# A decoder trunk on one core: the pre-norm's factor of each feature moves from the transposed input into the weights of the feed-forward parts

## The chip, the cores and the metric

The kernel runs on one core of a Trainium2 chip. The metric is the device time of one execution in microseconds, and the time before is the median of three runs. In what follows TensorE, VectorE, ScalarE, GpSimd and SyncE are the five engines of the core; the profile calls them PE (with PEld for its weight loads), DVE, ACT, POOL and SP.

## What is computed

Two layers act on 256 tokens of 1024 features in float32. A layer is a feed-forward part, a token mixer (a short convolution, sparse attention and attention into 256 memory tokens), and a second feed-forward part. The part that matters here is this:

```python
def rms_norm(x, g):
    y = x * lax.rsqrt(jnp.mean(x * x, axis=-1, keepdims=True) + EPS)
    return y * g                       # g: one factor for each of 1024 features

def swiglu(h, w_in, w_out):            # w_in 1024 x 5632, w_out 2816 x 1024
    a, b = jnp.split(h @ w_in, 2, axis=-1)
    return (jax.nn.silu(a) * b) @ w_out

for l in range(2):
    h = rms_norm(x, ffn1_norm_pre[l])
    x = x + 0.5 * rms_norm(swiglu(h, ffn1_w_in[l], ffn1_w_out[l]), ffn1_norm_post[l])
    h = rms_norm(x, mix_norm_pre[l])
    x = x + rms_norm(token_mixer(h, ...), mix_norm_post[l])
    h = rms_norm(x, ffn2_norm_pre[l])
    x = x + 0.5 * rms_norm(swiglu(h, ffn2_w_in[l], ffn2_w_out[l]), ffn2_norm_post[l])
```

The factor `g` multiplies the rows of `w_in` as well as it multiplies the columns of the normed input: `(y * g) @ w_in` is `y @ (g[:, None] * w_in)`.

## The kernel before

**Numbers in two pieces.** Each float32 operand of a matmul is split into a high piece (`hi`, rounded to the format that TensorE multiplies fast) and the rest (`lo`). A product is three matmuls into one PSUM bank: hi by hi, hi by lo, lo by hi. For weights this is `split_unit` (L280): ScalarE copies the loaded tile `raw` to `whi` (L286), and VectorE subtracts, `wlo = raw - whi` (L287). For activations it is done behind a transpose.

**Units of weights.** A unit is one tile of 128 partitions by 1024 columns (512 KB). In the feed-forward input product (`product`, L348) a unit is one k of eight (128 of the 1024 features) with 512 columns of `a` and 512 of `b`; five groups of columns are done so. The last 256 + 256 columns go through `halves` (L367): there a unit holds two k at once, so that it is again 1024 columns wide, and four units make the product. It uses `product2` (L361), which takes the two k one behind the other.

**Two streams.** The 256 tokens are two streams of 128, t = 0 and t = 1. Each runs through the layers in steps, and a loop (L1309) lets them step in turn, t = 1 some steps behind, so that both use the same unit of weights. A step of a feed-forward part is six matmuls of 512 columns.

**Order.** The program is run once dry to learn at which step each unit is asked for (its due time). In the real pass `prefetch` (L293) issues a unit's load up to 7 steps ahead of its due time (`LOADS`) and its split up to 4 steps ahead (`AHEAD`), as long as there is a free buffer: 4 for `raw` and 8 for the pairs of `whi` and `wlo`. Every unit counts as one buffer, whatever its width. SyncE's queue keeps this order. On the other engines the framework places instructions by its own planner, in which the order of the program is the priority, and it derives the waits; only in the first steps are instructions pinned to the order of the program (`pinned`, L175).

**The pre-norm.** `prenorm` (L446) transposes a stream's 128 x 1024 input on TensorE, four 128 x 128 blocks to a PSUM bank (`pt`, two banks). VectorE multiplies each half by the factors into `hf` (`gained`, L457), ScalarE copies that to `hThi` (L462), VectorE makes `hTlo` (L463). The reciprocal of the root mean square is applied later, behind the product. The call for the first part of all is `warm` (L465): it interleaves the two halves with the splits of the first two units, and the second half's factors are applied by ScalarE in four pieces (L454). Idle matmuls (`keep_clock`) stand beside it.

**Behind the product** comes `gate` (L537: ScalarE tanh L539, VectorE L540 and L544), and for every two groups of columns a transpose that goes through VectorE, DRAM and back (`turn`, L394), whose end is again a split (`turnhi` L423, `turnlo` L424). Then `output` (L516) multiplies by `w_out`, 22 units of one k by 1024 columns.

Of the kernel before, what the change touches and what calls it, by code (L numbers as in the profile page):

```python
# [24 lines left out]
AF = mybir.ActivationFunctionType  # L25
OP = mybir.AluOpType
AX = mybir.AxisListType

P = 128
# [28 lines left out]
ATT_A, ATT_B, ATT_C, ATT_D, ATT_T = 1, 3, 2, 6, 10  # L58
EARLY, RAMP, SCALES, STAGED = 6, 10, 5, 8
PACE, PACE_1, PACED = 9, 8, ("nsa", "memory")  # L60

PRE = ("ffn1_norm_pre", "mix_norm_pre", "ffn2_norm_pre", "mem_norm")

# [40 lines left out]
def view(ap, off, dims):  # L104
    if isinstance(ap, Nothing):
        return ap
    return bass.AP(tensor=ap.tensor, offset=ap.offset + off, ap=[list(ap.ap[0])] + [list(d) for d in dims])


def f32(ap):  # L110
    return ap.bitcast(F32)
# [19 lines left out]
def program(tc, nc, pools, a, out, plan):  # L131
# [18 lines left out]
    def bank(name):  # L150
        return psa.tile([P, 512], F32, name=name, tag="a")

    def tbank():
        return pst.tile([P, 512], F32, name="pt", tag="t")

    def gtile(name, dt=F32):
        return gp.tile([P, 1024], dt, name=name, tag="g")

    def ttile(name, dt=F32):
        return tp.tile([P, 520], dt, name=name, tag="tmp")  # L160
# [7 lines left out]
    def keep_clock(count):  # L168
        ps = bank("idle")
        for _ in range(count):  # L170
            pinned(nc.tensor.matmul(ps, lhsT=idle[:, :P], rhs=idle[:, :512], start=True, stop=True))
# [3 lines left out]
    def pinned(ins):  # L175
        if first_steps[0] and not dry:
            tc.keep_in_program_order(ins)
# [5 lines left out]
    for half in range(2):  # L183
        sl = slice(half * 512, (half + 1) * 512)
# [9 lines left out]
    gT = consts.tile([P, 64], F32, name="gT")  # L194
# [24 lines left out]
    def ask(kind, key, parts=None):  # L219
        if dry:  # L220
            if key not in found:
                found[key] = [now[0], kind, key, parts, 0]
                order.append(found[key])
            found[key][4] += 1
            return nc if kind == "g" else [nc, nc]
        if key not in ready:
            fetch(key)
        return ready[key]

    def unit(key, parts):  # L230
        hi, lo = ask("w", key, parts)
        later(0, lambda: drop("w", key))
        return hi, lo

    def drop(kind, key):
        if not dry:
            left[key] -= 1
            if left[key] == 0:
                free[kind] += 1
# [39 lines left out]

    def split_unit(between=None):  # L280
        item, raw, n = splits.pop(0)
        free["w"] -= 1
        hi = wp.tile([P, 1024], F32R, name="whi")
        lo = wp.tile([P, 1024], F32R, name="wlo")
        for c0, c1 in ((0, n),) if between is None else ((0, n // 2), (n // 2, n)):
            pinned(nc.scalar.copy(hi[:, c0:c1], raw[:, c0:c1]))  # L286
            pinned(nc.vector.tensor_sub(lo[:, c0:c1], raw[:, c0:c1], f32(hi[:, c0:c1])))  # L287
            if c0 == 0 and between is not None:
                between()
        ready[item[2]] = [hi, lo]  # L290
        free["raw"] += 1
# [41 lines left out]
    def later(delay, fn):  # L333
        serial[0] += 1
        deferred.append((now[0] + delay, serial[0], fn))
# [7 lines left out]
    def mm3(ps, xh, xl, wh, wl, start, stop, skip=False):  # L343
        nc.tensor.matmul(ps, lhsT=xh, rhs=wh, start=start, stop=False, skip_group_check=skip)  # L344
        nc.tensor.matmul(ps, lhsT=xh, rhs=wl, start=False, stop=False, skip_group_check=skip)  # L345
        nc.tensor.matmul(ps, lhsT=xl, rhs=wh, start=False, stop=stop, skip_group_check=skip)  # L346
# [14 lines left out]
    def product2(ps, x2, hi, lo, n, k0, first, last):  # L361
        for kk in range(2):
            k = k0 + kk
            mm3(ps[:, :n], x2[0][:, k], x2[1][:, k], hi[:, kk * n:(kk + 1) * n], lo[:, kk * n:(kk + 1) * n],
                first and kk == 0, last and kk == 1)

    def halves(hT, name, l, parts):  # L367
        ps = bank("acc")
        width = sum(n for _, n in parts)
        for u in range(4):  # L370
            hi, lo = unit((name, l, parts[0][0], u), [(i * n, width, name, l, 2 * u, 2, c, n)
                                                      for i, (c, n) in enumerate(parts)])
            product2(ps, hT, hi, lo, width, 2 * u, u == 0, u == 3)
            yield 0
        return ps
# [9 lines left out]
    def transpose4(src, c0, n=4):  # L385
        pt = tbank()
        for j in range(n):
            pinned(nc.tensor.transpose(pt[:, j * P:(j + 1) * P], src[:, c0 + j * P:c0 + (j + 1) * P], ident))  # L388
        return pt
# [52 lines left out]
    def tokens_last(hi, lo):  # L442
        r = "p (k t) -> p k t"
        return hi.rearrange(r, k=8), lo.rearrange(r, k=8)

    def prenorm(src, name, l, warm=False):  # L446
        hi, lo = gtile("hThi", F32R), gtile("hTlo", F32R)
        g0 = PRE.index(name) * 16 + l * 8
        hf = [ttile("hf") for _ in range(2)]

        def gained(half, pt):
            if warm and half == 1:
                for c in range(4):
                    pinned(nc.scalar.activation(hf[1][:, c * P:(c + 1) * P], pt[:, c * P:(c + 1) * P], AF.Copy,  # L454
                                                scale=gT[:, g0 + 4 + c:g0 + 5 + c]))
                return
            pinned(nc.vector.tensor_tensor(view(hf[half], 0, [[P, 4], [1, P]]), view(pt, 0, [[P, 4], [1, P]]),  # L457
                                           view(gT, g0 + half * 4, [[1, 4], [0, P]]), op=OP.mult))

        def halved(half):  # L460
            sl = slice(half * 512, (half + 1) * 512)
            pinned(nc.scalar.copy(hi[:, sl], hf[half][:, :512]))  # L462
            pinned(nc.vector.tensor_sub(lo[:, sl], hf[half][:, :512], f32(hi[:, sl])))  # L463

        if warm and splits:  # L465
            pts = []
            for half in range(2):
                pts.append(transpose4(src, half * 512))
                keep_clock(WARM[1 + half])
            gained(0, pts[0])  # L470
            split_unit(lambda: halved(0))
            split_unit()
            gained(1, pts[1])
            halved(1)
        else:
            for half in range(2):
                gained(half, transpose4(src, half * 512))
            for half in range(2):
                halved(half)
        scale = norm_scales(src, SCALES if first_steps[0] else 0)  # L480
        yield NORM_B
        return tokens_last(hi, lo), scale
# [731 lines left out]
    def mixer(t, l):  # L1214
# [3 lines left out]
        def columns(c0, n=512):  # L1218
            return halves(hT, "w_mix_in", l, [(c0, n)])
# [147 lines left out]
```

## Time and profile before

| | |
|---|---|
| median of 3 runs | 1257.37 us (1257.1 to 1258.28) |
| the profiled execution | 1259.41 us, of which 1257.7 us are the span from its first to its last instruction |
| TensorE, matmuls | 1242.4 us busy, 99% of the span |
| TensorE, weight loads | 1027.2 us, 82% |
| VectorE | 915.1 us, 73% |
| ScalarE | 725.6 us, 58% |
| GpSimd | 211.8 us, 17% |
| DMA | 286.85 MB, 228 GB/s in the mean |

Busy times are of the whole span. A stage has its own limit, and which wait ends last in a stage is read from its rows. A matmul's duration in the timeline is longer than its share of TensorE's time, since matmuls overlap; the distance from one start to the next is what counts.

### The profile page before, as it was taken

To read this page: it belongs to the slowest core of one execution; us is meant where nothing else is said; L and a number is where in the kernel's file an instruction comes from. 1 tells how busy PE (TensorE), PEld (TensorE's weight loads), DVE (VectorE), ACT (ScalarE), POOL (GpSimd) and SP (SyncE) were. 2 spreads that over 40 slices of the span, in tenths; PEclk is the share of its full clock that TensorE was granted. 3 is DMA by queue.
4 is the path that set the end of the run, shared out by engine and by line. 5 is a ranking of instruction groups with operands and counts; after the bars stand their busy time and mean duration, and the time that the engine had idled before them with its cause. 6 is when DMAs were issued, how large, how long until landed. Compare 5 with 4: busy or idle time off the path is not lost.

```text
span 1257.7 us, 16609 instructions
## 1 busy us (share of the span) xinstructions
PE 1242.4 (99%) x5775; PEld 1027.2 (82%) x5775; DVE 915.1 (73%) x1168; ACT 725.6 (58%) x1138; POOL 211.8 (17%) x413
## 2 busy tenths in 40 slices
PE   9999999999999999999999999999999999999997
PEld 6888888878887888888888888888888888888886
DVE  7767657888997686676576676678899876767753
ACT  6545545877875454554464545568867754645441
POOL 3011601402120011011011014024012200110110
PEclk9999999999999999999999999999999999999999
DMA  7877876776687657787757788758558877577871
GB/s 255 261 242 264 279 246 216 225 232 201 188 272 241 219 175 213 246 255 229 251 173 230 233 271 300 242 178 258 162 192 272 243 235 219 172 244 220 250 248 71
DMA packets 133907, 286.85 MB, mean 228 GB/s; under 512 B 11872, under 2 KB 30976, under 8 KB 133824
## 3 DMA queue, kind: packets, MB, share of 16 engines
q1 hardware_dynamic: 117984, 238.78, 60.9%
q0 software_dynamic: 15520, 46.49, 11.1%
q8 instruction: 45, 0.74, 0.2%
q10 hardware_dynamic: 320, 0.53, 0.1%
q14 instruction: 38, 0.31, 0.1%
HBM read 261.64 MB, written 24.12 MB: 227 GB/s over the span
## 4 chain that ended last, share of the span: by engine, by line
PE 81%; DVE 6%; DMA 5%; ACT 4%; issue 3%; POOL 1%; DVEq 0%; SPq 0%; POOLq 0%; ACTq 0%
PE acc L356 34%; PE y L346 7%; PE y L345 7%; PE y L344 7%; PE acc L346 6%; PE acc L344 6%; PE acc L345 6%; DVE wlo L287 2%; DMA moved<-there 2%; PE pt L388 1%; PE br L344 1%; PE br L346 1%; PE br L345 1%; ACT whi L286 1%; DMA there<-blocks 1%
## 5 line engine op out<-in xcount | busy, mean ns | idle before, releaser
L287 DVE TENSOR_TENSOR wlo<-raw,whi 128x1024 fp32r<-128x1024 f32 (+2 forms) x441 | 532.3, 1214 | 247.1 <-ACT whi L286 242.7
L286 ACT CAST whi<-raw 128x1024 fp32r<-128x1024 f32 (+2 forms) x441 | 456.9, 1043 | 371.3 <-PE acc L356 177.9
L356 PE MATMUL acc<-wlo,hThi 128*128 128x512 f32 x640 | 198.6, 390 | 0.0
L356 PE MATMUL acc<-whi,hThi 128*128 128x512 f32 x640 | 197.8, 391 | 0.3 <-ACT hThi L462 0.3
L356 PE MATMUL acc<-whi,hTlo 128*128 128x512 f32 x640 | 197.2, 389 | 0.0
L344 PE MATMUL acc<-whi,hThi 128*128 128x512 f32 (+1 forms) x480 | 187.5, 391 | 0.4 <-ACT hThi L462 0.4
L346 PE MATMUL acc<-whi,hTlo 128*128 128x512 f32 (+1 forms) x480 | 184.8, 385 | 0.1
L345 PE MATMUL acc<-wlo,hThi 128*128 128x512 f32 (+1 forms) x480 | 184.7, 385 | 0.0
L403 POOL DMA_DIRECT2D there<-blocks x184 | 101.1, 556 | 490.8 <-DVE blocks L398 408.7
L356 PEld LDWEIGHTS acc<-whi,hThi 128*128 128x128 f32 x640 | 119.9, 188 | 25.6 <-ACT hThi L462 0.7
L356 PEld LDWEIGHTS acc<-whi,hTlo 128*128 128x128 f32 x640 | 120.1, 188 | 25.2 <-DVE hTlo L463 0.4
L356 PEld LDWEIGHTS acc<-wlo,hThi 128*128 128x128 f32 x640 | 120.1, 188 | 25.3 <-DVE wlo L287 0.4
L346 PE MATMUL y<-whi,turnlo 128*128 128x512 f32 x352 | 137.3, 390 | 0.0
L345 PE MATMUL y<-wlo,turnhi 128*128 128x512 f32 x352 | 137.2, 390 | 0.0
L344 PE MATMUL y<-whi,turnhi 128*128 128x512 f32 x352 | 137.1, 389 | 0.0
L346 PEld LDWEIGHTS acc<-whi,hTlo 128*128 128x128 f32 x480 | 90.2, 188 | 18.5 <-DVE hTlo L463 0.6
L344 PEld LDWEIGHTS acc<-whi,hThi 128*128 128x128 f32 x480 | 90.3, 188 | 17.3 <-ACT hThi L462 1.3
L345 PEld LDWEIGHTS acc<-wlo,hThi 128*128 128x128 f32 x480 | 90.4, 188 | 15.1
L345 PEld LDWEIGHTS y<-wlo,turnhi 128*128 128x128 f32 x352 | 66.1, 188 | 13.7
L346 PEld LDWEIGHTS y<-whi,turnlo 128*128 128x128 f32 x352 | 66.1, 188 | 13.7
L344 PEld LDWEIGHTS y<-whi,turnhi 128*128 128x128 f32 x352 | 66.1, 188 | 13.6
L424 DVE TENSOR_TENSOR turnlo<-moved,turnhi 128x1024 fp32r<-128x1024 f32 (+1 forms) x42 | 49.2, 1171 | 31.0 <-ACT turnhi L423 31.0
(293 smaller groups left out, 1457.6 us busy)
## 6 DMA issues: line engine op xcount, KB each, us to landing
raw<-in_ffn_w_in_dram SPq DMA_DIRECT2D x159, 512.0 KB, 4.8
raw<-in_w_mix_in_dram SPq DMA_DIRECT2D x96, 512.0 KB, 4.5
raw<-in_ffn_w_out_dram SPq DMA_DIRECT2D x88, 512.0 KB, 4.6
there<-blocks POOLq DMA_DIRECT2D x152, 128.0 KB, 4.5
moved<-there POOLq DMA_DIRECT2D x38, 512.0 KB, 5.8
raw<-in_ffn_w_in_dram SPq DMA_DIRECT2D x33, 256.0 KB, 4.1
raw<-in_w_mem_kv_dram SPq DMA_DIRECT2D x16, 512.0 KB, 5.0
raw<-in_w_mix_out_dram SPq DMA_DIRECT2D x16, 512.0 KB, 4.4
```

What stands on the lines that cost most here:

```text
L286: pinned(nc.scalar.copy(hi[:, c0:c1], raw[:, c0:c1]))
L287: pinned(nc.vector.tensor_sub(lo[:, c0:c1], raw[:, c0:c1], f32(hi[:, c0:c1])))
L344: nc.tensor.matmul(ps, lhsT=xh, rhs=wh, start=start, stop=False, skip_group_check=skip)
L345: nc.tensor.matmul(ps, lhsT=xh, rhs=wl, start=False, stop=False, skip_group_check=skip)
L346: nc.tensor.matmul(ps, lhsT=xl, rhs=wh, start=False, stop=stop, skip_group_check=skip)
L356: pinned(nc.tensor.matmul(p[:, :n], lhsT=hT[x2][:, k], rhs=w[:, j * n:(j + 1) * n], start=(k == 0 and i == 0), stop=(k == 7 and i == 2)))
L388: pinned(nc.tensor.transpose(pt[:, j * P:(j + 1) * P], src[:, c0 + j * P:c0 + (j + 1) * P], ident))
L403: nc.gpsimd.dma_start(there[:, q * f:(q + 1) * f].rearrange("(p j) f -> j p f", j=32), blocks[q * 32:(q + 1) * 32, :n].rearrange("j (p f) ...
L424: nc.vector.tensor_sub(lv, mv, f32(hv))
```

## The change

The factors of the two feed-forward pre-norms are multiplied into `w_in` where its units are split: ScalarE's copy becomes an activation with a factor for each partition, and VectorE's subtraction becomes `raw * factor - whi` in one instruction. For this a unit must hold one k, so the units of `halves` are made half as wide (8 of 512 columns in place of 4 of 1024), with the same matmuls in the same order and a step for every two of them. The feed-forward pre-norms lose `hf`: ScalarE and VectorE split the transposed input straight from PSUM. In the `warm` call the second half is split before the second unit instead of behind it. The mixer's pre-norm stays as it was, apart from code that it doesn't reach.

```diff
+FOLDED = {"ffn1_w_in": "ffn1_norm_pre", "ffn2_w_in": "ffn2_norm_pre"}

     def split_unit(between=None):
         item, raw, n = splits.pop(0)
+        gains = None
+        if item[2][0] in FOLDED:
+            k = PRE.index(FOLDED[item[2][0]]) * 16 + item[2][1] * 8 + item[2][3]
+            gains = gT[:, k:k + 1]
...
         for c0, c1 in ((0, n),) if between is None else ((0, n // 2), (n // 2, n)):
-            pinned(nc.scalar.copy(hi[:, c0:c1], raw[:, c0:c1]))
-            pinned(nc.vector.tensor_sub(lo[:, c0:c1], raw[:, c0:c1], f32(hi[:, c0:c1])))
+            if gains is None:
+                pinned(nc.scalar.copy(hi[:, c0:c1], raw[:, c0:c1]))
+                pinned(nc.vector.tensor_sub(lo[:, c0:c1], raw[:, c0:c1], f32(hi[:, c0:c1])))
+            else:
+                pinned(nc.scalar.activation(hi[:, c0:c1], raw[:, c0:c1], AF.Copy, scale=gains))
+                pinned(nc.vector.scalar_tensor_tensor(lo[:, c0:c1], raw[:, c0:c1], gains, f32(hi[:, c0:c1]),
+                                                      op0=OP.mult, op1=OP.subtract))
...
     def halves(hT, name, l, parts):
         ps = bank("acc")
         width = sum(n for _, n in parts)
+        if name in FOLDED:
+            for k in range(8):
+                hi, lo = unit((name, l, parts[0][0], k), [(i * n, 0, name, l, k, 1, c, n)
+                                                          for i, (c, n) in enumerate(parts)])
+                mm3(ps[:, :width], hT[0][:, k], hT[1][:, k], hi[:, :width], lo[:, :width], k == 0, k == 7)
+                if k % 2:
+                    yield 0
+            return ps
...
     def prenorm(src, name, l, warm=False):
-        hf = [ttile("hf") for _ in range(2)]
+        hf = None if name in FOLDED.values() else [ttile("hf") for _ in range(2)]
         def gained(half, pt):
-            if warm and half == 1:
-                for c in range(4):
-                    pinned(nc.scalar.activation(hf[1][:, c * P:(c + 1) * P], pt[:, c * P:(c + 1) * P], AF.Copy,
-                                                scale=gT[:, g0 + 4 + c:g0 + 5 + c]))
-                return
...
-        def halved(half):
+        def halved(half, pt=None):
             sl = slice(half * 512, (half + 1) * 512)
-            pinned(nc.scalar.copy(hi[:, sl], hf[half][:, :512]))
-            pinned(nc.vector.tensor_sub(lo[:, sl], hf[half][:, :512], f32(hi[:, sl])))
+            src = hf[half][:, :512] if pt is None else pt
+            pinned(nc.scalar.copy(hi[:, sl], src))
+            pinned(nc.vector.tensor_sub(lo[:, sl], src, f32(hi[:, sl])))

         if warm and splits:
...
-            gained(0, pts[0])
-            split_unit(lambda: halved(0))
+            split_unit(lambda: halved(0, pts[0]))
+            halved(1, pts[1])
             split_unit()
-            gained(1, pts[1])
-            halved(1)
+        elif hf is None:
+            for half in range(2):
+                halved(half, transpose4(src, half * 512))
         else:
```

## Rows read from the trace of the kernel before

**Rows 1.** Page, part 1: busy us (share of the span) xinstructions

```profile
PE 1242.4 (99%) x5775; PEld 1027.2 (82%) x5775; DVE 915.1 (73%) x1168; ACT 725.6 (58%) x1138; POOL 211.8 (17%) x413
```

**Rows 2.** Busy us of each engine (x instructions), clock, DMA share, GB/s, one stretch

```profile
100.00:200.00 100.00, 100.00 (x442) 82.45 (x441) 64.95 (x65) 50.39 (x58) 28.23 (x52) 1.00 0.81 271
```

**Rows 3.** Who TensorE waited for, whole span: us in total, times, longest

```profile
PE acc L344 <- ACT hThi L462: 0.4, 2, 0.2
PE acc L356 <- ACT hThi L462: 0.3, 1, 0.3
```

**Rows 4.** Waits of all engines, whole span: us in total, times, longest

```profile
DVE wlo L287 <- ACT whi L286: 242.7, 225, 2.9
ACT whi L286 <- PE acc L356: 177.9, 132, 2.2
```

**Rows 5.** Timeline of TensorE's matmuls in the first steps (start, us)

```profile
9.87 1.06 PE L388 MATMUL pt<-ident,x 128*128 128x128 f32 x8 [0.85 <-DMA x<-in_x_dram]
10.69 0.71 PE L356 MATMUL acc<-whi,hThi 128*128 128x512 f32 x2
...
12.61 0.73 PE L356 MATMUL acc<-whi,hThi 128*128 128x512 f32 x2 [0.28 <-ACT hThi L462]
...
17.39 0.62 PE L356 MATMUL acc<-whi,hThi 128*128 128x512 f32 x2
```

**Rows 6.** Chain that ended last, in order of time, first steps (start, us)

```profile
11.31 0.61 DVE hf L457
...
11.94 0.63 ACT hThi L462
```

**Rows 7.** Timeline of SyncE, first steps, and landing times of L267, first 14 us

```profile
3.04 56.85 SPq L267 DMA_DIRECT2D raw<-in_ffn_w_in_dram  x26
...
DMA to landing us min/median/max: 4.7/6.1/8.6
```

**Rows 8.** Groups by line and shape: count, busy us, mean ns, idle before and releasers

```profile
L287 DVE TENSOR_TENSOR wlo<-raw,whi 128x1024 fp32r<-128x1024 f32 x431 | 525.1, 1225 | 246.3 <-ACT whi L286 241.9 <-PE acc L356 0.5
L286 ACT CAST whi<-raw 128x1024 fp32r<-128x1024 f32 x431 | 450.7, 1053 | 369.6 <-PE acc L356 177.9 <-PE y L346 85.9 <-PE acc L346 48.4
...
L511 DVE SCALAR_TENSOR_TENSOR x<-pn,nr,x 128x512 f32<-128x512 f32 x24 | 17.0, 749 | 1.3 <-POOL nr L439 0.4
...
L457 DVE TENSOR_TENSOR hf<-pt,gT 128x512 f32<-128x512 f32 x23 | 15.2, 686 | 1.5 <-PE pt L388 0.9
...
L925 ACT ACTIVATE p<-p,rg 128x256 f32<-128x256 f32 x32 | 13.7, 505 | 2.2 <-DVE rg L810 2.2
...
L379 ACT CAST mThi<-pt 128x512 fp32r<-128x512 f32 x8 | 4.7, 584 | 2.9 <-PE pt L388 2.9
```

**Rows 9.** TensorE around `halves` of the second feed-forward part, layer 0

```profile
555.97 0.39 PE L344 MATMUL acc<-whi,hThi 128*128 128x512 f32 x1
...
562.76 0.39 PE L344 MATMUL acc<-whi,hThi 128*128 128x512 f32 x1
...
566.85 0.39 PE L344 MATMUL y<-whi,turnhi 128*128 128x512 f32 x1
```

**Rows 10.** ScalarE and VectorE in the same stretch

```profile
561.26 1.05 ACT L423 CAST turnhi<-moved 128x1024 fp32r<-128x1024 f32 x1 [1.78 <-DMA moved<-there]
...
564.32 1.05 ACT L286 CAST whi<-raw 128x1024 fp32r<-128x1024 f32 x1 [0.48 <-PE acc L346]
...
562.35 1.23 DVE L424 TENSOR_TENSOR turnlo<-moved,turnhi 128x1024 fp32r<-128x1024 f32 x1 [1.60 <-ACT turnhi L423]
...
565.34 0.75 DVE L544 SCALAR_TENSOR_TENSOR wide<-th,rs,acc 128x512 f32<-128x512 f32 x1
```

**Rows 11.** SyncE: loads of these units; then their issues, min/median/max ns; then landing

```profile
533.57 9.09 SPq L276 DMA_DIRECT2D raw<-in_ffn_w_in_dram  x8
...
L276 SPq DMA_DIRECT2D raw<-in_ffn_w_in_dram x32: 367/425/1475, 94.7 to 1163.9; - x32
...
raw<-in_ffn_w_in_dram SPq DMA_DIRECT2D x33, 256.0 KB, 4.1
```

## The prediction, made before the change was run

> **What bounds the kernel now.** The page comes first: TensorE's matmuls are busy for 1242.4 of 1257.7 us, VectorE for 915.1, ScalarE for 725.6 [rows 1]. So no engine that the change relieves or loads has to be the bound, and only 15.3 us of the span are without a matmul. The next view, the busy times of a stretch, says whether busy means full: in 100 us of a feed-forward part 442 matmuls start, one every 0.2262 us, with no idle time [rows 2]. I use 0.2262 as the cadence; a step (six matmuls) is 1.357 us, and a unit of weights, used by both streams, lasts 2.71 us.
>
> Then the waits: of the waits of TensorE for what the pre-norm makes (`hThi`), the whole span has 0.3 us in the feed-forward parts (L356) and 0.4 us at L344 [rows 3], which in a feed-forward part is never the first to read it: that is the mixers. The longest waits are of other engines: VectorE for ScalarE's copy, 242.7 us, and ScalarE for TensorE, 177.9 us in 132 waits [rows 4]. The last is to be read so: the split of a unit waits until stream 1 has used the unit eight before it, because there are eight buffers. Splitting runs ahead as far as the buffers allow, and TensorE sets its pace. What is left to win or lose is where TensorE stands still: in the first steps, and wherever the change makes it wait.
>
> **The first steps.** TensorE transposes stream 1's input at 9.87 us, held up by the landing of `x` [rows 5]; the change can't move that. Stream 0's second unit follows at 10.69 and needs six matmuls: to 12.05. But stream 1's first product starts at 12.61, and three steps later it is 17.39 [rows 5]. From 12.05 to 17.39 are 5.34 us for 18 matmuls, which take 4.07: 1.27 us are lost. The chain shows why: `hf` on VectorE at 11.31, then `hThi` on ScalarE from 11.94 to 12.57, then the matmul [rows 6].
>
> With the change `hf` is gone, and ScalarE reads PSUM: 0.584 us for 128x512 (L379) [rows 8]. The first half of the transposes ends at about 10.28 (half of 9.87 to 10.69), `hThi` at 10.86, `hTlo` (a VectorE instruction on PSUM of this size, 0.686 by L457 [rows 8]) at 11.55, before it is needed at 12.05. Late next is the third unit of weights. Its load is issued at 3.04 and lands at most 8.6 us later, at 11.64 [rows 7]; ScalarE's copy takes to 12.78, VectorE's rest to 14.07 (durations below). Stream 0 needs them at 13.41 and 14.31. They are in time by 0.24 us. I take a gain of 1.2; the bounds are 0.56 (only the wait up to 12.61 goes, the rest belongs to the weights) and 1.27.
>
> **The seven other feed-forward pre-norms.** They lose 14 VectorE multiplications of 0.686 us, but TensorE waits nowhere in the feed-forward parts for `hThi` but in the start [rows 3]: the other stream's matmuls cover it. I take nothing; a gain is excluded by that row, and a loss too, since each chain gets shorter. The PSUM bank `pt` is held until `hTlo` is made, 0.584 us longer a half than until `hf` was; the other stream's next transposes come steps later.
>
> **The splits.** There are 160 units of 1024 columns in `product`, and `halves` has 32 units of 512 in place of 16 of 1024. No row shows a copy from SBUF with a factor for each partition at this size. The nearest is L925: 0.505 for 256 columns [rows 8]. A plain copy takes 1.053 for 1024 [rows 8] and 0.63 for 512 [rows 6], 0.83 ns a column, so 0.42 for 256: the factor costs 0.09. By that a split copy takes 1.14, a half one 0.72. Between nothing and four times L925 (2.02, were all of it to grow with the columns) I take 0.09, because a plain copy has a fixed part too: 0.63 for 512 columns is more than half of 1.053. On VectorE the three-operand form with a factor for each partition took 0.749 (L511) against 0.686 for two operands: 0.06 more, 1.29 a unit, 0.75 a half one; twice L511, 1.50, is the upper bound.
>
> The work that hides this is TensorE's 2.71 us for each unit. In the stretch of rows 2 ScalarE was busy for 50.39 us and VectorE for 64.95; with 37 units (442/12) the values add 3.3 and 2.2, the upper bounds 36 and 10. Both engines stay under 90 of 100, so either way it costs nothing on the path. Over the kernel VectorE gets 160 x 0.06 + 32 x 0.75 - 16 x 1.225 - 15 x 0.686 = 3.7 us more to do.
>
> **The narrow units: buffers.** Here something gets worse. A buffer counts as a unit whatever its width, so in `halves` eight buffers hold four steps of weights and not eight. Stream 1 runs five steps behind (562.76 against 555.97 [rows 9]). I number the narrow units 0 to 7 and follow the second feed-forward part of layer 0.
>
> Unit 7 takes the buffer of `product`'s last unit. Stream 1 has that step from 560.05 (two steps before 562.76) and is done with `whi` after four matmuls, 560.95. A release reaches ScalarE 0.2 us later (the step from 562.76 ends at 564.12, the copy starts at 564.32 [rows 9, 10]): 561.15. If `turnhi` is ahead of it as now, to 562.31, and `turnlo` on VectorE to 563.58 [rows 10], the copy ends at 563.03 and the rest at 564.33. Needed: 565.02, the second matmul of the second half of the step that starts at 555.97 + 6 x 1.357. Margin 0.7.
>
> The first unit of `w_out` takes unit 0's buffer, free at 562.76 + 3 x 0.226 + 0.2 = 563.64. Behind unit 7 ScalarE has the gate's tanh, VectorE its two products; at 0.75 each (L544 [rows 10]) the copy ends at 564.83 and the rest at 564.33 + 1.50 + 1.22 = 567.05. TensorE asks for it with the second matmul of `output`, 566.85 [rows 9] + 0.23 = 567.08. That is no margin. Behind the waiting split stand the next splits and the next gate, whose users come later, so a delay is paid once for each of the four stages. If VectorE takes the split ahead of the gate it costs 0; if one more instruction of 1.23 us (`turnlo`) slips in front, 1.2. I take 0.1 for a stage, nearer to the order worked out, 0.4 in all; the ends are 0 and 4.8.
>
> **The narrow units: loads.** 64 loads of 128 KB stand in place of 32 of 256 KB. SyncE issues one in 0.37 to 0.43 us and its queue started these 22.4 us before their use (533.57 against 555.97) [rows 9, 11]. GpSimd's queue is not passed or touched. Of four `raw` buffers each is taken for 4.1 us of landing (that of twice the size) [rows 11] + 0.72 + 0.75 = 5.6 us; four units are used up in 5.43. That loses 0.15 us in four units, 0.3 in a stage, against a lead of 22.4 us: nothing.
>
> The Trainium skill speaks against the narrow loads ("DMA: Bandwidth & Descriptors", section "Rules for kernel authors": at least 1 MiB a transfer for full bandwidth; its section "Anatomy of one DMA" gives a fixed 2.0 us each, for the software path). By its figure two transfers in series would cost 2 us more; were that exposed once in each of four stages, 8 us, an estimate from that page. The trace shows the cover that the rule does not count, so the sum leaves it out.
>
> **Sum.** -1.2 + 0.4 = -0.8 us. The profiled execution would be 1259.4 - 0.8 = 1258.6; the runs' median lies 2.0 below it, so 1257.4 - 0.8 = 1256.6. This measurement can tell about 0.2%, 2.5 us, from no change.
>
> **Rivals.**
> 1. The start's gain is not kept. For: the first units come straight from the loads, and the next ones too have to land before TensorE gets to them; or the loads of the narrow units are short by 0.3 us a stage. Against: 0.24 us of margin and the lead above. Then -1.2 is 0 and the time 1257.4 to 1257.8.
> 2. The buffers run out (the slower side). Place: unit 7 and the first units of `w_out`, on VectorE's queue. Price 1.2 a stage, 4.8 - 1.2 = +3.6: 1261.0. It decides, past 0.2%, from 0.93 us a stage. For: the margin of nothing. Against: the other instructions there have later users, so the planner need not put them first.
> 3. The planner, which places instructions by its own durations, orders the mixers' queues otherwise. For: the mixers' work shares ScalarE and VectorE with the splits, and what runs ahead of it gets other durations. Against: nothing in the mixers is edited. TensorE's whole idle time is 15.3 us [rows 1], of which I let it move 3 either way: 1253.6 or 1259.6 and more.
> 4. TensorE is not the limit. If the splits set the pace, VectorE's 3.7 us are paid: 1261.1. Against it are ScalarE's 177.9 us of waiting for TensorE [rows 4] and the even cadence [rows 2]. The Trainium skill ("Perfetto Trace Analysis", section "Identifying the Most-Contended Engine") says that matmul busy time is a bad measure and weight-load busy time a good one; that is 82%, which would leave TensorE 18% of room. Here the loads too start once every 0.227 us without a break (441 in 100 us, 82.45 us busy [rows 2]), so the room is the gap of each pair, and the measured cadence decides.
>
> **How the numbers follow.** The forecast has 0.62, rival 1 0.14, rival 2 0.09, rival 3 0.12 (0.07 faster, 0.05 slower), rival 4 0.03. The forecast and rival 1 lie within 0.2%: 0.76. Faster 0.07, slower 0.09 + 0.05 + 0.03 = 0.17. The range goes from 1255.0, below the full start gain (1256.1) and some of rival 3, to 1260.5, which takes in about half of rival 2; left out are 0.07 below and some 0.11 above.
>
> **What would show it.** At the start the matmul after the second unit starts near 12.05, and the start now at 17.39 comes near 16.2. `whi` takes 1.14, `wlo` 1.29. In rows like 2 the cadence stays 0.226. At the first `output` matmul after `halves` TensorE waits for `wlo` between 0 and 0.3 us, four times. The prediction is wrong if that wait is near 1 us or longer, if the splits are much dearer than their bounds, or if TensorE's idle time in the mixers changes by more than 2 us.

## The result and the profile after

The changed kernel takes 1266.39 us (median of four executions, 1264.39 to 1269.17), the kernel before 1257.44 beside it: 1.0068 times as long, 95% interval [1.0056, 1.0079]. I had forecast 1256.6 and a range up to 1260.5. It is slower by 9.0 us, and the range missed it.

The profiled execution is one of the shorter ones, 1264.94 us; its span is 5.5 us longer than that of [rows 1]. Its page:

```profile
span 1263.2 us, 16733 instructions
...
PE 1243.5 (98%) x5775; PEld 1027.8 (81%) x5775; DVE 916.2 (73%) x1169; ACT 743.6 (59%) x1150; POOL 207.1 (16%) x413
```

TensorE has 1.1 us more of busy time and 4.4 us more without a matmul. No engine has become full. Stretches show where; first three of the kernel before (start:end, TensorE's busy time and its matmuls, then the other engines, the granted clock, DMA share and GB/s):

```profile
10.00:20.00 10.00, 9.71 (x44) 7.21 (x44) 8.21 (x18) 8.64 (x16) 4.00 (x8) 1.00 0.70 239
...
100.00:130.00 30.00, 30.00 (x134) 24.84 (x133) 21.98 (x24) 15.72 (x17) 4.39 (x9) 1.00 0.82 276
130.00:170.00 40.00, 40.00 (x178) 33.06 (x177) 25.89 (x27) 20.70 (x27) 21.66 (x40) 1.00 0.87 296
```

and of the changed one, with the row that answers to [rows 2]:

```profile
10.00:20.00 10.00, 9.97 (x48) 8.45 (x49) 8.49 (x16) 8.73 (x15) 5.27 (x9) 1.00 0.85 277
...
100.00:200.00 100.00, 97.23 (x423) 79.95 (x422) 64.15 (x66) 50.37 (x61) 26.66 (x51) 0.98 0.80 262
100.00:130.00 30.00, 30.00 (x134) 24.84 (x133) 19.86 (x24) 14.60 (x19) 3.49 (x7) 1.00 0.70 213
130.00:170.00 40.00, 37.23 (x158) 30.34 (x157) 25.34 (x27) 20.27 (x26) 20.43 (x39) 0.96 0.93 320
700.00:800.00 100.00, 98.37 (x434) 80.80 (x433) 66.36 (x69) 50.46 (x61) 20.61 (x40) 1.00 0.78 258
```

The start gained four matmuls, 0.9 us. Where the last columns of layer 0's first feed-forward part are multiplied and the next weights loaded (100 to 130), TensorE is as full as before, but the DMA moves 213 GB/s, not 276. Behind it (130 to 170) the DMA is fuller than before, 320 against 296, and there 20 matmuls are missing; in the whole 100 us it is 19, or 4.3 us. In the other layer (700 to 800) the kernel before starts 443 and this one 434: 2.0 us. These less the start's 0.9 make 5.4 of the 5.5 us.

The waits of TensorE say for what it stood still:

```profile
PE pt L651 <- DMA stage<-in_cmp_v_b_dram: 2.8, 1, 2.8
...
PE acc L355 <- ACT mThi L682: 1.5, 2, 0.9
...
PE acc L357 <- DVE mTlo L683: 0.8, 1, 0.8
```

None is for weights. `stage` holds small tables for the mixer, loaded by GpSimd; `mThi` and `mTlo` are the memory input, which too goes through transfers on GpSimd's queue. Neither is touched by the diff. The chain of the changed kernel leads from there back to the feed-forward part (start, us, what):

```profile
126.50 1.06 ACT whi L293
...
129.21 1.02 DVE wlo L294
130.26 0.98 DVE blocks L417
...
133.16 7.44 DMA there<-blocks
...
141.18 5.43 DMA moved<-there
...
147.90 3.67 DMA stage<-in_cmp_v_b_dram
151.57 0.33 issue
151.90 0.27 PE pt L651
```

GpSimd's queue works in order: the last `stage` load stands behind `moved`, and `moved` behind the landing of `there`. The queue in the kernel before:

```profile
129.93 2.18 POOL L403 DMA_DIRECT2D there<-blocks  x4 [12.64 <-DVE blocks L398]
...
136.65 0.58 POOL L410 DMA_DIRECT2D moved<-there  x1 [2.51 <-DMA there<-blocks]
...
143.85 0.50 POOL L631 DMA_DIRECT2D stage<-in_cmp_v_b_dram  x1
```

and in the changed one:

```profile
131.53 2.18 POOL L422 DMA_DIRECT2D there<-blocks  x4 [17.46 <-DVE blocks L417]
...
141.18 0.58 POOL L429 DMA_DIRECT2D moved<-there  x1 [5.45 <-DMA there<-blocks]
...
147.90 0.50 POOL L647 DMA_DIRECT2D stage<-in_cmp_v_b_dram  x1
```

The last load is issued 4.05 us late (147.90 against 143.85). The queue is late already when it begins: `there` is issued 1.60 us later (131.53 against 129.93). Its data, `blocks`, are made by VectorE behind the gate's last `th`, before:

```profile
127.69 0.42 DVE L540 SCALAR_TENSOR_TENSOR th<-th,acc 128x256 f32<-128x256 f32 x1
...
128.66 0.98 DVE L398 STREAM_TRANSPOSE blocks<-wide 128x768 f32<-128x768 f32 x1
```

and after:

```profile
127.15 0.41 DVE L556 SCALAR_TENSOR_TENSOR th<-th,acc 128x256 f32<-128x256 f32 x1
127.59 1.23 DVE L294 TENSOR_TENSOR wlo<-raw,whi 128x1024 fp32r<-128x1024 f32 x1
```

Behind this `wlo` come `wide` and a second `wlo`, and then `blocks` at 130.26 (the chain above): two splits of `w_out` stand in the gate's way, and from `th` to `blocks` it is 3.11 us in place of 0.97. The rest of the lateness is the transfer: from `there` to `moved` are 9.65 us in place of 6.72. What the transfers share the DMA with is seen on SyncE's queue, before:

```profile
94.70 9.05 SPq L276 DMA_DIRECT2D raw<-in_ffn_w_in_dram  x8
105.59 19.84 SPq L276 DMA_DIRECT2D raw<-in_ffn_w_out_dram  x8
```

and after:

```profile
93.87 18.88 SPq L278 DMA_DIRECT2D raw<-in_ffn_w_in_dram  x16
114.67 16.03 SPq L278 DMA_DIRECT2D raw<-in_ffn_w_out_dram  x8
```

The loads of the last columns, the same bytes, take 20.8 us to the next load instead of 10.9. The loads of `w_out` start 9.1 us later and then go faster than before, just when `there`, `moved` and `stage` need the DMA. In 130 to 150 us of the changed kernel a transfer took, median from issue to landing:

```profile
raw<-in_ffn_w_out_dram SPq DMA_DIRECT2D x8, 512.0 KB, 6.7
m<-in_mem_dram SPq DMA_DIRECT2D x2, 512.0 KB, 8.0
there<-blocks POOLq DMA_DIRECT2D x8, 96.0 KB, 6.3
```

Before, in the same stretch, these were 4.6, 5.4 (one load) and 4.8 us.

**Theory A**, formed here: eight narrow pairs of `whi` and `wlo` hold half the columns that eight wide ones hold. The splits, and so the loads, cannot run as far ahead; the loads then catch up in a burst, and the burst delays the mixer's small transfers behind it, for which TensorE waits. The two splits ahead of `blocks` are not part of theory A; the table of experiment 3 has them beside it. The rivals are the folding itself (dearer splits, no `hf`), the smaller transfers, and the narrow units as such, wherever they stand.

### The profile page after: what moved, and what is told of

Same layout as the page of the kernel before. It is cut to its first block, busy times and chain, and to the rows that moved or that the text cites. A ratio compares the mean times of both kernels' runs of the same rounds, so it can differ in the third digit from the quotient of the medians.

```text
span 1263.2 us, 16733 instructions
## 1 busy us (share of the span) xinstructions
PE 1243.5 (98%) x5775; PEld 1027.8 (81%) x5775; DVE 916.2 (73%) x1169; ACT 743.6 (59%) x1150; POOL 207.1 (16%) x413
## 4 chain that ended last, share of the span: by engine, by line
PE 79%; DMA 8%; DVE 5%; ACT 4%; issue 2%; POOL 1%; SPq 0%; DVEq 0%; POOLq 0%; ACTq 0%
PE acc L367 34%; PE acc L357 7%; PE acc L355 7%; PE acc L356 7%; PE y L356 5%; PE y L357 5%; PE y L355 5%; DMA there<-blocks 3%; DMA moved<-there 2%; PE pt L407 1%; PE br L355 1%; PE br L356 1%; PE br L357 1%; DVE wlo L294 1%; ACT whi L293 1%
## 5 line engine op out<-in xcount | busy, mean ns | idle before, releaser
L294 DVE TENSOR_TENSOR wlo<-raw,whi 128x1024 fp32r<-128x1024 f32 (+1 forms) x264 | 316.4, 1211 | 96.5 <-ACT whi L293 94.3
L293 ACT CAST whi<-raw 128x1024 fp32r<-128x1024 f32 (+1 forms) x264 | 270.6, 1039 | 149.4 <-PE acc L357 43.6
L297 DVE SCALAR_TENSOR_TENSOR wlo<-raw,gT,whi 128x1024 fp32r<-128x1024 f32 (+1 forms) x193 | 229.1, 1189 | 150.4 <-ACT whi L296 147.9
L296 ACT ACTIVATE whi<-raw,gT 128x1024 fp32r<-128x1024 f32 (+1 forms) x193 | 207.2, 1077 | 213.9 <-PE acc L367 184.7
```

Source lines behind the costliest of these rows:

```text
L296: pinned(nc.scalar.activation(hi[:, c0:c1], raw[:, c0:c1], AF.Copy, scale=gains))
L297: pinned(nc.vector.scalar_tensor_tensor(lo[:, c0:c1], raw[:, c0:c1], gains, f32(hi[:, c0:c1]), op0=OP.mult, op1=OP.subtract))
```

## Experiments

All ratios are to runs of the kernel before on the same chip, with 95% intervals.

**1. Which part of the change.** One kernel has the factors in the weights but keeps the last columns in wide units, each split in two copies and two rests with their own factors:

```diff
+        if name in FOLDED and col == 2560:
+            cuts = ((0, 512), (512, 1024))       # two k of a wide unit
...
+                k = PRE.index(FOLDED[name]) * 16 + l * 8 + (2 * u + c0 // 512 if col == 2560 else u)
```

> The factors stay in the weights, but the units of the last columns keep two k and 1024 columns; their split is two copies and two rests, each with its own factors. Theory A (the narrow units delay the loads, and these come later in a burst that holds up the other transfers): 1256.6, within 1255.5 to 1257.5, no wait of TensorE for the small transfers (stage), and no dip of TensorE's clock near 155 us. Theory B (the dearer splits cost the time, 1.15 and 1.28 us in place of 1.05 and 1.23): 1262 to 1267 as with the change. Theory C (the pre-norm without hf places other work otherwise): also 1262 to 1267.

It took 1256.36 us, 0.9996 [0.9987, 1.0006]. With more executions:

> The version with the factors in the weights and wide units, timed in more rounds: is its start gain of 0.8 us to be seen in the time? Sum of the terms: -0.8 us, 0.9993 of the time before; 0.9985 to 1.0003 would fit the gain and also no difference, so only an interval wholly below 1 settles that it beats the kernel before. The rival, that the dearer splits cost something: 1.0005 or more.

1257.83 us, 0.9996 [0.9988, 1.0005]: whether the start's gain remains can't be told from nothing, but the folding costs nothing. The counterpart is the kernel before with narrow units and nothing else (the plain copy, `hf` kept):

```diff
+        if name in ("ffn1_w_in", "ffn2_w_in"):
+            for k in range(8):
+                hi, lo = unit((name, l, parts[0][0], k), [(i * n, 0, name, l, k, 1, c, n)
+                                                          for i, (c, n) in enumerate(parts)])
```

> The kernel before with nothing but the narrow units (8 of 512 columns in place of 4 of 1024 in the last columns of the feed-forward input product); the factors stay in the pre-norm. Theory A: 1263 to 1270, TensorE waits about 2 to 4 us near 150 us for the small transfers. Theories B and C: 1257.4, no such wait.

1263.59 us, 1.004 [1.0018, 1.0061], and the same picture as in the changed kernel, in the waits of TensorE

```profile
PE pt L643 <- DMA stage<-in_cmp_k_b_dram: 1.7, 1, 1.7
```

and in the two stretches:

```profile
100.00:130.00 30.00, 30.00 (x134) 24.86 (x133) 18.91 (x24) 14.13 (x20) 3.73 (x7) 1.00 0.68 212
130.00:170.00 40.00, 38.27 (x170) 31.41 (x169) 25.59 (x27) 20.69 (x27) 20.38 (x40) 1.00 0.94 323
```

A third kernel takes `hf` away alone: the kernel before with the feed-forward pre-norms split straight from PSUM. It leaves out these norms' factors.

```diff
+        elif hf is None:
+            for half in range(2):
+                halved(half, transpose4(src, half * 512))
```

> The kernel before with the feed-forward pre-norms split straight from PSUM, and the factors of these two norms left out altogether: no factor in the splits, no narrow units. Theory A: 1256.2 to 1256.8 (the gain of the first steps alone). Theory B: the same. Theory C: 1262 or more.

1257.6 us, 1.0002 [0.9989, 1.0016]: no loss, and the start's gain that I had expected here does not show either. So the loss belongs to the narrow units, which cost 0.40% alone where the changed kernel costs 0.68%.

**2. Where they harm.** Wide units in one of the two feed-forward parts, narrow in the other:

```diff
-        if name in FOLDED and col == 2560:
+        pair = name in FOLDED and name != NARROW and col == 2560     # NARROW: "ffn1_w_in" or "ffn2_w_in"
```

> The factors are in the weights in both feed-forward parts, but only the first feed-forward part of each layer keeps the narrow units; the second one uses wide units of two k. Theory A (the narrow units halve the columns loaded ahead, the loads of the output weights then come in a burst, and the mixer's small transfers behind it on GpSimd's queue come too late): a mixer follows these parts, so the whole loss stays: 1263 to 1267 us, TensorE waits 2 to 3 us for the stage's transfer, DMA at about 213 GB/s in 100 to 130 us and 320 GB/s in 130 to 170 us. Rival (narrow units cost the same wherever they stand, by their more and smaller instructions and transfers): half the loss, about 1261 us here and in the kernel with narrow second parts.

> The counterpart: narrow units only in the second feed-forward part of each layer, wide ones in the first. Theory A: the loads dip and catch up in a burst there too, but no mixer's transfers stand behind it, so nothing is lost: 1256 to 1257.5 us, no wait of TensorE for the stage's transfer, TensorE at full cadence in 130 to 170 us. Rival (the cost is of the units themselves): about 1261 us.

Narrow in the first parts: 1263.54 us, 1.0046 [1.003, 1.0062]. In the second: 1257.67, 0.9999 [0.9989, 1.0009]. The same units cost 0.46% or nothing, by what stands behind them: only the first parts are followed by a mixer's transfers. The dip is there in the second parts too: the loads of the last columns take 20.8 us to the next load (532.37 to 553.17) for 10.9 before (533.57 to 544.45), the DMA moves 199 GB/s in 530 to 560 us for 258, and `there` lands in 6.7 us for 4.8 (565 to 600 us); yet TensorE starts 134 matmuls in each 30 us from 530 to 620, as before. That excludes a price of the units as such.

**3. Which resource.** The kernel before, each unit of the last columns loaded in four transfers of 128 KB instead of two of 256 KB:

```diff
+                loads4 = [(kk * width + i * n, 0, name, l, 2 * u + kk, 1, c, n)
+                          for kk in range(2) for i, (c, n) in enumerate(parts)]
```

> The kernel before with its wide units, but each unit of the last columns is loaded by four transfers of 128 KB in place of two of 256 KB; buffers, splits and matmuls are those of before. Theory A (it is the number of columns that the buffers hold, not the transfers' size): no change, 1257 to 1258 us, DMA near 275 GB/s in 100 to 130 us. Rival (smaller transfers bring less bandwidth, as the Trainium skill's page on DMA would have it): 1261 us or more, and DMA well under 276 GB/s in 100 to 130 us.

1258.1 us, 0.9998 [0.9988, 1.0008], 268 GB/s in 100 to 130 us. It is not the size of the transfers. The Trainium skill ("DMA: Bandwidth & Descriptors", section "Rules for kernel authors") asks for at least 1 MiB a transfer for full bandwidth; this run shows no loss in going from 256 to 128 KB.

Then the two kinds of buffers apart, both with the factors in the weights. Wide `raw` split into two narrow pairs:

```diff
+            free["w"] -= 2
+            for c0 in (0, 512):
+                hi = wp.tile([P, 1024], F32R, name="whi")
+                lo = wp.tile([P, 1024], F32R, name="wlo")
```

> Factors in the weights; the last columns are loaded as wide units of two k, as before, but split into two narrow pairs of whi and wlo, each in a buffer of its own. Only the eight pairs count by narrow units here, the four raw buffers hold as much as before. If the pairs are the short ones (stream 1 releases a pair five steps after stream 0 took it, and eight narrow pairs hold four steps): the loss stays, 1262 to 1267 us, DMA near 213 GB/s in 100 to 130 us and 320 GB/s in 130 to 170 us, TensorE waits for the stage's transfer or the memory input. If the raw buffers are the short ones: 1256 to 1258 us and 275 GB/s.

and two narrow `raw` split into one wide pair:

```diff
+            free["raw"] -= 2
+            for kk in range(2):
+                raw = rawp.tile([P, 1024], F32, name="raw")
```

> The counterpart: the last columns are loaded as narrow units, each in a raw buffer of its own (64 loads of 128 KB, as in the changed kernel), and two of them are split into one wide pair. Only the raw buffers count by narrow units. If the pairs are the short ones: 1256 to 1258 us, DMA near 270 GB/s in 100 to 130 us, no wait for the stage's transfer. If the raw buffers are: 1262 to 1267 us and 213 GB/s.

Narrow pairs: 1262.21 us, 1.0038 [1.0024, 1.0052], with theory A's waits of TensorE

```profile
PE acc L375 <- ACT mThi L701: 3.1, 1, 3.1
...
PE pt L670 <- DMA stage<-in_cmp_v_b_dram: 1.5, 1, 1.5
```

and its dip and catching up:

```profile
100.00:130.00 30.00, 30.00 (x134) 24.83 (x133) 19.14 (x23) 14.89 (x19) 5.15 (x10) 1.00 0.62 199
130.00:170.00 40.00, 38.52 (x171) 31.61 (x170) 27.05 (x30) 21.21 (x28) 22.48 (x39) 1.00 0.91 319
```

Narrow `raw`: median 1259.73 us, but from 1256.93 to 1271.89 in ten executions, 1.0031 [1.0009, 1.0054]; the profiled one, at 1256.93, shows no dip (273 GB/s). That is neither of the two answers that I had expected. Once more:

> Narrow raw buffers, wide pairs, as in narrow_raw, in more rounds. If the raw buffers cost nothing and the spread of the first ten runs was not the kernel's: 1256.5 to 1258 us, interval around 1. If they carry a part of the loss: 1259 to 1261 us again, wholly above 1, and the profile shows waits of TensorE that the kernel with wide units has not.

1258.4 us, 1255.61 to 1270.74, 1.0025 [1.0002, 1.0048]: eight of twelve up to 1259, four from 1263. Of these 22 executions eight are above 1262 us; of the 104 of the kernel before on the four chips of experiments 1 to 4 five are, so the kernel before has such executions too, but far fewer. So three single executions, each with its trace:

> Narrow raw buffers and wide pairs once more, for the profile of one execution each (three looks). If an execution above 1262 us is among them: by theory A its loss lies where a mixer's small transfers are late (TensorE waits for the stage's transfer or for mThi and mTlo, 2 us or more, in 130 to 200 us or 750 to 850 us, and after it a stretch of granted clock of 0.50). By the rival (the narrow loads themselves are late) TensorE waits for whi or wlo in the feed-forward parts. If all three are near 1257 us, this stays open.

They took 1258.18, 1262.99 and 1258.57 us. In the long one TensorE waits

```profile
PE acc L370 <- ACT mThi L689: 4.9, 1, 4.9
```

and SyncE's queue reads:

```profile
93.91 15.28 SPq L260 DMA_DIRECT2D raw<-in_ffn_w_in_dram  x16
109.46 18.02 SPq L289 DMA_DIRECT2D raw<-in_ffn_w_out_dram  x8
```

The narrow `raw` buffers delay the next loads too, by 3.9 us (109.46 against 105.59) where the changed kernel has 9.1, and in this execution the place where it is paid is again the mixer's memory input. But the late loads alone do not make an execution long: the two others have them as well (15.5 us for the narrow ones in that of 1258.18) and wait at most 1.0 us for `mThi`, and so has the one of 1256.93 (109.49). What differs is on GpSimd's queue, in the long one:

```profile
149.34 1.27 POOL L512 TENSOR_SCALAR rs<-nr 128x1 f32<-128x1 f32 x1
...
151.81 1.06 POOL L515 TENSOR_SCALAR rs<-nr 128x1 f32<-128x1 f32 x1
...
152.93 0.60 POOL L429 DMA_DIRECT2D there<-blocks  x1
```

These are three instructions on 128 numbers, which stand ahead of a `there` of the memory input. In the execution of 1256.93 they take 0.26, 0.20 and 0.21 us, here 1.27, 1.04 and 1.06, while VectorE makes three `wlo` one behind the other (149.31 to 152.80). That `there` is issued at 152.93 in place of 148.93; 2.7 of the 4.0 us arise in these instructions. The same happens in the profiled executions with narrow pairs (1.09 and 1.06 us for two of them) and with narrow first parts (1.29 and 1.06): these two also wait for `mThi` in layer 0, 3.1 and 2.5 us, while in the changed kernel and with narrow units alone all three take 0.26 us or less there, and neither waits for `mThi` in layer 0. So the pairs carry the constant part of the loss. What the narrow `raw` buffers cost is a few long executions; the one that was traced is long mostly by where GpSimd's instructions fall, and that the narrow `raw` buffers bring this about is not shown.

These rows side by side, each of the profiled execution (GB/s in 100 to 130 us; from `th` to `blocks` on VectorE, us; from the first `there` after 125 us to the first `moved` after 130 us, us; when this `moved` is issued):

| kernel | narrow | GB/s | `th` to `blocks` | `there` to `moved` | `moved` | ratio |
|---|---|---|---|---|---|---|
| before | nothing | 276 | 0.97 | 6.72 | 136.65 | 1 |
| factors in the weights, wide units | nothing | 275 | 0.97 | 6.35 | 135.79 | 0.9996 |
| small transfers | transfers | 268 | 0.96 | 6.98 | 137.05 | 0.9998 |
| narrow second parts | not here | 279 | 0.96 | 6.59 | 136.01 | 0.9999 |
| narrow `raw` | `raw` | 273 | 0.96 | 7.08 | 136.65 | 1.0031 |
| narrow pairs | pairs | 199 | 3.12 | 9.04 | 142.23 | 1.0038 |
| narrow units alone | both | 212 | 3.12 | 9.49 | 141.42 | 1.0040 |
| narrow first parts | both | 214 | 3.11 | 8.32 | 139.95 | 1.0046 |
| changed | both | 213 | 3.11 | 9.65 | 141.18 | 1.0068 |

The four kernels with narrow pairs have all three: the dip, two splits ahead of `blocks`, and a slower `there`. Why the planner puts the splits there was not tried.

**4. What waits on the late transfers.** The changed kernel with the transpose of `stage` four steps later:

```diff
-        later(STAGED, turn)
+        later(STAGED + 4, turn)
```

> The changed kernel with the transpose of the small transfers (stage) put off by 4 more steps, 5.4 us. If the wait for them with its dip of the clock is the bulk of the loss, it goes: about 4.4 us less than the change, 1260 to 1262, and the rest of the loss is in the layer after. If the wait is a symptom of a late queue that holds up something else as well, less than 2 us of it go.

1261.93 us, 1.0037 [1.0022, 1.0052]: TensorE waits for `stage` no more, 130 to 170 us is full again, and about half of the loss is gone. The rest is now at the memory input:

```profile
PE acc L355 <- ACT mThi L682: 2.7, 2, 2.4
```

Then the changed kernel with the start of the whole setup (`stage`, the memory input) five steps later, meant to come behind the burst:

```diff
-            if k == 4 and t == 0 and which == 1:
+            if k == 9 and t == 0 and which == 1:
                 begin_layer(l)
```

> The changed kernel with one move: the start of the mixer's setup (its small transfers and its product of the memory input) is issued at the ninth step of the first part's output product and not at the fourth, so behind the burst of loads. Theory A: TensorE's waits for the stage's transfer and for the memory input's pieces mostly go, and most of the loss with them: 1257 to 1260 us. Rival (the loss is TensorE's clock or the units themselves, and not the order on GpSimd's queue): 1264 to 1267 us. If the move only makes the setup late, the same waits stay or grow, and the time is over 1266 us.

1264.58 us, 1.0046 [1.0025, 1.0067]. I had expected 1257 to 1260, and that did not come. The `stage` wait is gone, but the memory input is now later than its user in both layers:

```profile
PE acc L355 <- ACT mThi L682: 6.6, 2, 3.3
```

Its control:

> A control for the run with the later setup: the kernel before with the same move (the mixer's setup issued at the ninth step of the output product and not at the fourth). If the move itself makes the memory input late: 1260 us or more, with TensorE's waits for mThi and mTlo; then the changed kernel's 1264.6 with the move holds the move's own loss. If the move costs nothing by itself: 1257 to 1258 us, and the changed kernel's waits there come from its late transfers.

The kernel before with the same move took 1254.62 us, 0.9978 [0.9965, 0.9991], and has no wait for `mThi` at all. So the move makes nothing late by itself; the narrow units do. Here they do it by lateness more than by slow transfers: from `there` to `moved` the two traces differ little (7.12 and 9.16 us with narrow units, 6.33 and 8.76 without), but the load of the memory input is issued at 142.53 and not at 138.97, VectorE makes its `blocks` at 159.64 and not at 153.30, and the first `mThi` comes at 182.23 and not at 172.73. That the move gains 2.8 us I had not expected. Again, and together with the factors in wide units:

> The kernel before with the later setup, once more beside the other two: 1254 to 1255.5 us, 0.9965 to 0.999, if the gain of 0.22% was no accident of a chip; 1257 us if it was.

> Factors in the weights, wide units, and the mixer's setup issued at the ninth step of the output product. If the late transfers of the narrow units were what spoiled the move in the changed kernel: the move's gain of 2.8 us and the start's 0.8 add up, 1253.5 to 1255 us, 0.997 to 0.9985, no wait for mThi or for the stage's transfer above 1 us. If the folding of the factors itself spoils it: 1257 us or more.

1256.09 us, 0.9982 [0.9967, 0.9997], and 1255.91 us, 0.9987 [0.9973, 1.0]. The kernel before with the later setup is thus faster than both kernels, by some 0.2% in both runs; with the folding it is no better. Both took a little longer than I had expected (1254 to 1255.5, and 1253.5 to 1255). Why the move gains was not tried.

## Why the prediction was wrong

**The start** was right in mechanism, and near in size. The matmul that I had put near 12.05 starts at 12.33, of which 0.16 is a later landing of `x`; the one of 17.39 [rows 5] starts at 16.41, 0.98 us earlier where I took 1.2.

**The other pre-norms** are nothing, as taken (1.0002 without `hf` and factors).

**The splits** were sized well and are hidden. I had 1.14 and 0.72 for ScalarE, 1.29 and 0.75 for VectorE; VectorE took 1.28 and 0.75, and ScalarE's groups by form show 1.15 and 0.73 (mean ns behind the busy time):

```profile
L296 ACT ACTIVATE whi<-raw,gT 128x1024 fp32r<-128x1024 f32 x159 | 182.5, 1152 | 167.4 <-PE acc L367 138.2 <-PE y L357 15.0 <-DVE wlo L297 5.7
L296 ACT ACTIVATE whi<-raw,gT 128x512 fp32r<-128x512 f32 x34 | 24.7, 725 | 46.5 <-PE acc L367 46.5
```

**The narrow units: buffers.** The pairs do run out: experiment 3 shows it, where narrow pairs alone bring the dip. The second row agrees with it (ScalarE idle for 46.5 us before the half-wide copies, all of it for TensorE to release a pair), but does not prove it, since the wide copies of the first row wait in the same way (138.2 us). That the pairs are short was seen. The margin of nothing at unit 7 and at the first unit of `w_out` cost nothing in 100 to 130 us, and no wait for weights in these parts is among the three new ones. What failed is the sentence that behind the waiting split stand splits "whose users come later", so that "a delay is paid once". Those users were matmuls only. The load that waits for the split's `raw` buffer was not followed, and neither was the gate: its `blocks`, behind two splits of `w_out`, come 1.60 us late and with them the first `there` on GpSimd's queue.

**The narrow units: loads** is the step that failed: "against a lead of 22.4 us: nothing". It reckoned the loads' pace from the `raw` buffers alone, 5.6 us for four units, so some 11 us for eight; it was 20.8. A `raw` buffer is free only when a split has a pair, and in this stage that happens at TensorE's pace with half the columns a pair; each kind of narrow buffer alone costs less here (15.7 us with narrow `raw` and wide pairs; 12.6 us with wide `raw` and narrow pairs, where the next eight loads then take 24.2 us for 19.8). And it compared the lead with TensorE's need for weights only. The lead did cover that. What it didn't cover was what the loads then collide with. "GpSimd's queue is not passed or touched" was true of the diff and false of the DMA that this queue shares, and of VectorE's order ahead of it. In place of nothing the runs show 0.38% with narrow pairs alone (1.0038, some 4.8 us) and 0.68% in the changed kernel.

**Rivals.** Rival 2 had the right buffers, and VectorE's order of splits and gate does change there, but its payer was wrong: TensorE does not wait for these weights. Rival 3 had the right payer, work for the mixers, and the planner's order is a part of it (the splits ahead of `blocks`), but the dip and the burst of the loads are not, and its price of 3 was too small. Rivals 1 and 4 did not happen. The sign that I had named, TensorE's idle time in the mixers changing by more than 2 us, is near to what the profile shows: 4.4 us, of which 2.8 are waits for the mixer's `stage` in the output product before it.

**Open.** The profile accounts for 5.5 of 9.0 us. The other 3.5 are executions: the profiled one of the kernel before was 2.0 us above its median (1259.41 against 1257.44), and this one 1.5 below its own (1264.94 against 1266.39); the longest took 4.2 us more than this one and was not seen in detail. That these too wait for the memory input is argued from other kernels' traces only. Narrow units alone cost 0.40% and the changed kernel 0.68%, with intervals that touch; what the factors add to the narrow units is not settled. Of the 4.05 us by which the last `stage` load is late, 1.60 arise on VectorE and 2.93 between `there` and `moved`, less 0.48 behind it; what each would cost alone is not shown, since no kernel had the one without the other. That the burst slows `there` rests on the transfers' times to landing, and with the later setup lateness is enough for the wait for the memory input, at little slower transfers.

## What to carry to other kernels

A pool that counts tiles, whatever their width, loses lead when tiles get narrower: count what the buffers hold in time, and follow a split that waits for a buffer on to the loads that wait for its source. A lead that covers the engine's need can still turn into a burst later; look at what shares the DMA there, above all short transfers on an in-order queue that have little margin, and at which instructions the splits now stand ahead of. To keep a per-partition factor, split the wide tile in two instructions rather than take two tiles.

## What was unexpected of the hardware

TensorE's longest stall here cost more than itself. After the 2.77 us without a matmul at 151.90, the granted clock of the changed kernel was, in stretches of 2 us:

```profile
150.00:152.00 2.00, 0.10 (x2) 0.13 (x2) 0.00 (x0) 1.93 (x2) 1.79 (x6) 1.00 0.59 165
152.00:154.00 2.00, 2.00 (x9) 1.58 (x10) 1.79 (x4) 0.00 (x0) 1.92 (x4) 0.84 0.94 368
154.00:156.00 2.00, 2.00 (x6) 1.56 (x5) 2.00 (x3) 0.98 (x2) 1.99 (x3) 0.50 0.67 149
156.00:158.00 2.00, 2.00 (x9) 1.60 (x7) 2.00 (x3) 0.90 (x1) 1.42 (x5) 0.81 0.98 387
```

The 0.50 is the lower of its two levels, 1.2 GHz for 2.4; in 158 to 160 it is 1.00 again. From 152.97 to 157.07 eleven matmuls started in 4.10 us in place of 2.49: 1.6 us on top of the wait. The later setup's 3.3 us wait in the changed kernel was followed by the same (0.50 in 194 to 196 us), and the 4.9 us wait of the long execution by 0.57 and 0.58 (178 to 182 us); the 1.5 us wait for `stage` in the kernel with narrow pairs was not (1.00 in 152 to 158).

GpSimd's smallest instructions can last as long as VectorE's beside them. In experiment 3 the three `rs` of the long execution end at 150.61, 151.74 and 152.87, right behind three `wlo` of 1.2 us each. In the kernel before one of them takes 0.20 us at 147.31, and 1.04 us at 152.78, while VectorE makes `wlo` (150.27 to 153.76). The transfers behind them on GpSimd's queue wait as well (4.0 us later in experiment 3, 2.7 of them so).
